# Two tiles for the turned residual, other places for two rounded sums, and filling that is counted from the first head

## The chip, the cores and the metric

The program runs on one core of one Trainium2 chip. The time is device microseconds of one execution, from the first to the last instruction with what lies around them. Before the change three runs gave 1033.18, 1035.9 and 1036.19 us, with a median of 1035.9.

## The reference, cut to what matters

Two layers over 512 tokens of width 1024, in float32: attention, an MLP, a recurrent block, an MLP, and a last norm. Every part is a residual branch behind an RMS norm.

```python
def sq_relu_mlp(h, w1, w2):
    z = jax.nn.relu(jnp.einsum('bsd,df->bsf', h, w1))
    return jnp.einsum('bsf,fd->bsd', z * z, w2)

for layer in range(DEPTH):
    hn = rmsnorm(h, norm_mix[layer])
    mix = chunked_band_attention(hn, ...) if layer % 2 == 0 else rglru_block(hn, ...)
    h = h + mix
    h = h + sq_relu_mlp(rmsnorm(h, norm_mlp[layer]), mlp_w1[layer], mlp_w2[layer])
return rmsnorm(h, norm_final)
```

With 512 tokens in chunks of 64 and eight chunks to the left, attention's band is the whole past: 16 heads of width 64, a bias per head by clipped distance, a softmax, and the output projection. The MLP goes up to 4096 and back.

## The kernel before

**Products in three parts.** Each float32 operand is split into a rounded high part (float32r) and what is left, and each product is made of three matmuls (`mm3`, lines 288 to 290). ScalarE casts the high part (for weights line 179, tiles wh), VectorE subtracts it for the low part (line 184, tiles wl). Weights come by DMA through a few raw tiles and a ring of five split tiles.

**Attention (lines 364 to 640).** The residual lies transposed: eight tiles of 128 features by 512 tokens. A loop runs over the heads: `score` (the two matmul lines 483 and 484, bias, maximum, exponent, scaling), one head later `turn` (ten transposes on TensorE, line 514), and another head later `weigh` (lines 529 and 530). Scores, transposes and the first two value tiles take turns in four PSUM banks with the tag "at". Between these three stands other matmul work: a queue of value, query and key projections and of the output projection, cut into steps of three matmuls. `fill(n)` adds n to a credit that may carry over at most 3, and takes steps from the queue while the credit is above 0; each step costs 2. `need` takes steps without regard to the credit where a head cannot do without a projection. Before the loop, 17 steps are taken directly. A key projection ends with `k_out`, which splits the key and copies it to the other 64 partitions by DMA on SP (lines 401 and 402).

**The MLP (`mlp`, line 681).** It uses products of 2 x 2 blocks with fewer multiplications, in Winograd's manner: sums of blocks of the weights (made on VectorE, or by accumulating DMAs that GpSimd issues) against sums of blocks of the input. At the start, `first` does four plain up tiles (`up`, j = 0 to 3), 24 matmuls of 512 columns each. Beside them:

- after the first tile, `turn` transposes the residual in 32 x 32 blocks on VectorE (line 744, 16 instructions) into the tile `turned`, and 32 DMAs (line 751, 16 on SP, 16 on GpSimd's queue) write it to `res`, where tokens lie on partitions;
- after the second, ScalarE scales the residual in its place by the norm's gain (line 697);
- after the third, `right` makes four sums of blocks of it (lines 701 to 705);
- after the fourth, `right_split` rounds them into rH (line 714, ScalarE) and rL (line 715, VectorE).

Then `group` runs seven products of 24 matmuls of 256 columns: the first on the plain operand (hnH, hnL), the second, third, fifth and seventh on the sums rH and rL. Between the first and the third stands a copy from PSUM to PSUM on ScalarE (line 850).

**Places.** The tile rH holds all four rounded sums, 16 KB in each partition, and has the tag "rH" that `turned` has: both take turns in one place, so the first cast into rH has to wait until all 32 DMAs have read `turned`. The low parts of sums 2 and 4 lie in the place of the residual's lower half, which sums 1 and 3 are read from. The two halves of a "22" block of the down weights have 8 KB under the tag "b22" and are loaded in `load_down`.

**Order.** A scheduler places the instructions on the engines by its own estimate of times, within what data and places allow; each engine and each DMA queue then works strictly in that order.

Of the kernel before, what the change touches and what calls it, by code (L numbers as in the profile page):

```python
# [10 lines left out]
F32 = mybir.dt.float32  # L11
F32R = mybir.dt.float32r
# [3 lines left out]
P = 128  # L16
T = 512
D = 1024
KT = D // P
NH = 16  # L20
HD = 64
U = 256
EPS = 1e-6
NEG = -1e30

FILL = 7.6

WARM = 10

# [6 lines left out]
def f(ap):  # L36
    return ap.bitcast(F32)
# [3 lines left out]
def trunk(ctx: ExitStack, tc: tile.TileContext, xT, cols, gfin, win, wqkv, wo, rwin, rga, rgx, rwo, w1, w2, out):  # L41
# [70 lines left out]
    def load_down(key, name):  # L112
        if key not in down:
            return
        both = state["raw"].tile([P, 2, 1024], F32, name=f"b{name}_{key[0]}{key[1]}", tag=f"b{name}")
        for h in range(2):
            raws[name, h] = both[:, h]
            nc.sync.dma_start(two(raws[name, h]), rows(down[key][name][h * U : (h + 1) * U]))
# [19 lines left out]
    def fetch():  # L138
        i = state["next"]
        state["next"] += 1  # L140
        kind, nk, key = plan[i]
        H = wsp.tile([P, 1024], F32R, name=f"wh{i}", tag="wh")
        L = wsp.tile([P, 1024], F32R, name=f"wl{i}", tag="wl")
# [34 lines left out]
        if i:  # L178
            high = S.copy(H[:, :n], raw[:, :n])  # L179
            if kind in ("us1", "us3", "t1", "t4") or kind in ("t2", "t3") and key[1] == 3:  # L180
                tc.keep_in_program_order(high)
        else:
            start_.append(V.tensor_copy(H[:, :n], raw[:, :n]))
        low = V.tensor_sub(L[:, :n], raw[:, :n], f(H[:, :n]))  # L184
        if not i:
# [24 lines left out]
        elif kind == "t4" and half:  # L210
            first_sum(following)
            load_down(following, "22")
            load_down(following, "21")
        state["ready"].append((nk, H[:, :n].rearrange("p (k c) -> p k c", k=nk), L[:, :n].rearrange("p (k c) -> p k c", k=nk)))

# [150 lines left out]
    with ExitStack() as actx:  # L366
# [6 lines left out]
        def bias_of(g):  # L373
            b = ab.tile([P, 4, T], F32, name=f"bias{g}", tag="bias")
            nc.sync.dma_start(b[:, :, 2 * P :], win[4 * g : 4 * g + 4].rearrange("h p j -> p h j"))
            for h in range(4):
                G.tensor_copy(b[:, h, 0 : 2 * P], b[:, h, 2 * P : 2 * P + 1].to_broadcast([P, 2 * P]))
            G.memset(b[0:HD, :, T - HD :], NEG)
            biases[g] = b
# [12 lines left out]
        def k_out(p, acc):  # L392
            tmp = a2.tile([P, T], F32, name=f"tk{p}", tag="tmp")
            V.tensor_mul(tmp, acc, r0)
            for hh in range(2):
                own, oth = HALF[hh], HALF[1 - hh]
                kh = ab.tile([P, T], F32R, name=f"kh{p}{hh}", tag=f"kh{hh}", bufs=2)
                kl = ab.tile([P, T], F32R, name=f"kl{p}{hh}", tag=f"kl{hh}", bufs=2)
                S.copy(kh[own], tmp[own])
                V.tensor_sub(kl[own], tmp[own], f(kh[own]))  # L400
                nc.sync.dma_start(f(kh[oth]), f(kh[own]))
                nc.sync.dma_start(f(kl[oth]), f(kl[own]))
                kk[2 * p + hh] = (kh, kl)
# [69 lines left out]
        def score(h):  # L473
            kh, kl = kk[h]
            s0, s1, s2 = atp(f"s0{h}"), atp(f"s1{h}"), atp(f"s2{h}")
            sc = [s0[:, 0:P], s0[:, P : 3 * P], s1[:, : 3 * P], s2]
            pt = a2.tile([P, 10 * P], F32, name=f"p{h}", tag="p")
            mx = a2.tile([P, 4], F32, name=f"mx{h}", tag="mx")
            sm = a2.tile([P, 4], F32, name=f"sm{h}", tag="sm")
            b = biases[h // 4]  # L480
            for t in range(4):
                n = (t + 1) * P
                PE.matmul(sc[t], q[h][:, t * P : n], kl[:, :n], start=True, stop=False)
                PE.matmul(sc[t], q[h][:, t * P : n], kh[:, :n], start=False, stop=True)
            for t in range(4):
                n = (t + 1) * P
                V.tensor_tensor_reduce(
                    out=pt[:, seg[t] : seg[t] + n], in0=sc[t], in1=b[:, h % 4, T - n :],
                    scale=1.0, scalar=-3.0e38, op0=ALU.add, op1=ALU.max, accum_out=mx[:, t : t + 1],
                )  # L490
            V.tensor_scalar(mx, mx, -1.0, None, ALU.mult)
            for t in range(4):
                n = (t + 1) * P
                S.activation(
                    pt[:, seg[t] : seg[t] + n], pt[:, seg[t] : seg[t] + n], AF.Exp,
                    bias=mx[:, t : t + 1], accum_out=sm[:, t : t + 1],
                )
            V.reciprocal(sm, sm)
            for t in range(4):
                n = (t + 1) * P  # L500
                V.tensor_scalar(pt[:, seg[t] : seg[t] + n], pt[:, seg[t] : seg[t] + n], sm[:, t : t + 1], None, ALU.mult)
            pts[h] = pt
# [90 lines left out]
        credit = [0]  # L593

        def step():
            try:
                credit[0] -= next(queue[0][1])
            except StopIteration:
                queue.pop(0)
# [6 lines left out]
        def need(name):  # L606
            while any(name == item[0] for item in queue):
                step()
# [3 lines left out]
        q_out(1, accs[1])  # L612
        for _ in range(KT):
            step()
        for i in range(NH + 2):
            if i < NH:
                if i % 4 == 0 and i > 0:
                    bias_of(i // 4)
                if i >= 4:
                    need(f"k{i // 2}")  # L620
                score(i)
                if i == 0:
                    k_out(1, accs[3])
                at["s"] = i
            fill(FILL)
            if 0 <= i - 1 < NH:
                turn(i - 1)
            fill(FILL)
            if 0 <= i - 2 < NH:
                if i == 15:  # L630
                    need("woA")
                need(f"v{(i - 2) // 8}")
                weigh(i - 2)
                if i == 9:
                    residual("h")
                    for k in range(KT):
                        nc.sync.dma_start(hT[k], xT[k * P : (k + 1) * P, :])
                at["w"] = i - 2
            fill(FILL)
        need("woB")  # L640
# [40 lines left out]
    def mlp(ly, norm):  # L681
        with ExitStack() as mctx:
            sr, zp, dp = (mctx.enter_context(tc.tile_pool(name=f"{n}{ly}", bufs=1)) for n in ("sr", "z", "d"))
# [2 lines left out]
            xs = [(hnH[k], hnL[k]) for k in range(KT)]  # L686
            res = dp.tile([P, 4, 2, T], F32, name=f"d{ly}", tag="d")
            dt = {(t, c): res[:, t, c] for t in range(4) for c in range(2)}
            turned = zp.tile([P, 2, 2, 4, KT, 32], F32, name=f"turned{ly}", tag="rH")
            rights = []  # L690
            rL13 = zp.tile([P, 2, 4, U], F32R, name=f"rL13{ly}", tag="rL")
            low_, high = hB[0], hB[1]
            rF = {1: low_[:, :, LO], 3: low_[:, :, HI], 4: high[:, :, LO], 2: high[:, :, HI]}
            rL = {1: rL13[:, 0], 3: rL13[:, 1]}
# [10 lines left out]
                    V.scalar_tensor_tensor(rF[n], rF[1 if n == 2 else 2], -1.0, rF[n], ALU.mult, ALU.subtract)  # L705

            def right_split(n):
                if n == 1:
                    rights.append(zp.tile([P, 4, 4, U], F32R, name=f"rH{ly}", tag="rH"))
                if n == 2:  # L710
                    rL24 = per.tile([P, 2, 4, U], F32R, name=f"rL24{ly}", tag="hx0")
                    rL.update({2: rL24[:, 0], 4: rL24[:, 1]})
                H = rights[0][:, n - 1]
                S.copy(H, rF[n])  # L714
                V.tensor_sub(rL[n], rF[n], f(H))  # L715

            def operand(n):
                if n[0] == "r":
                    H, L = rights[0][:, int(n[1]) - 1], rL[int(n[1])]
                    return [(H[:, k], L[:, k]) for k in range(4)]  # L720
                ks, c = (range(4) if n[0] == "1" else range(4, KT)), (LO if n[1] == "1" else HI)
                return [(hnH[k][:, c], hnL[k][:, c]) for k in ks]
# [15 lines left out]


            def turn():  # L740
                blocks = [turned[:, h] for h in range(2)]
                for k in range(KT):
                    for h in range(2):
                        V.transpose(
                            blocks[h].rearrange("p t j k a -> p (t j) k a")[:, :, k],
                            hT[k][:, h * U : (h + 1) * U].rearrange("p (n b) -> p n b", b=32),
                        )
                for h in range(2):
                    for i in range(4):
                        for j in range(4):  # L750
                            (G if j % 2 else nc.sync).dma_start(
                                res[32 * j : 32 * j + 32, 2 * h : 2 * h + 2, i // 2, (i % 2) * U : (i % 2 + 1) * U],
                                blocks[h][32 * i : 32 * i + 32, :, j].rearrange("p t k a -> p t (k a)"),
                            )
# [327 lines left out]
    def open_x(u):  # L1082
        WH, WL = want(1)
        for i in range(2):
            xbs.append(mmp(f"xb{2 * u + i}"))
            project(xbs[-1:], PAIR[i : i + 1], WH, WL, [(hnH[k], hnL[k]) for k in range(4, KT)], last=False)
            yield

    mlp(0, nm1)


    nm2 = Norm("nm2", C_MLP1, late=True)
    with ExitStack() as rctx:
# [142 lines left out]
        for u in range(2, 4):  # L1236
            WH, WL = want(2)
            for i in range(2):
                m = 2 * u + i
                project([accs[m]], PAIR[i : i + 1], WH, WL, [gd[k] for k in range(KT)])  # L1240
                ro_out(m)

    mlp(1, nm2)


# [39 lines left out]
```

## Time and profile before

| | |
|---|---|
| profiled execution | 1035.93 us, its span 1034.2 us |
| granted TensorE clock | 0.999 |
| PE (matmuls) busy | 1021.6 us, 99% |
| VectorE busy | 866.8 us, 84% |
| ScalarE busy | 665.7 us, 64% |
| GpSimd busy | 99.4 us, 10% |
| attention's head loop | about 40 to 229 us of the span |
| first MLP, recurrent block, second MLP | from about 244, 555 and 709 us |

PE is TensorE's matmuls, PEld its weight loads, DVE VectorE, ACT ScalarE, POOL GpSimd, SPq the DMA queue of SyncE. A row of a timeline gives the start, the duration, the engine, the line, the operation, the tile written and the tiles read, and in brackets how long the engine stood idle before it and what ended that. Shown durations of matmuls overlap. Tile names stand without their numbers: `m` is a bank of `group`, `s` one of scores, `x` in line 514 one of transposes, `v` of values.

### The profile page before, as it was taken

How to read it: one execution, taken by the hardware profiler on the slowest of the kernel's cores; microseconds unless marked ns; L12 is line 12 of the kernel's file. 1: busy time of each engine (PE TensorE's matmuls, PEld its weight loads, DVE VectorE, ACT ScalarE, POOL GpSimd, SP SyncE). 2: the span in 40 equal slices, each digit the busy share in tenths (PEclk: the TensorE clock that was granted, in tenths of full speed). 3: DMA queues.
4: the chain of work that ended last, by engine and by line, in shares of the span. 5: the costliest groups of instructions: out<-in, count | busy, mean ns of one | idle time of the engine just before them, and what ended most of it. 6: DMA issues, size and time to landing. Idle time of an engine off the chain costs nothing.

```text
span 1034.2 us, 15261 instructions
## 1 busy us (share of the span) xinstructions
PE 1021.6 (99%) x5762; PEld 892.5 (86%) x5762; DVE 866.8 (84%) x1222; ACT 665.7 (64%) x1020; POOL 99.4 (10%) x128
## 2 busy tenths in 40 slices
PE   9999999999999999999999999999999999999997
PEld 7888888888999999999988788888899999999986
DVE  7998778869789898698688989977789698698687
ACT  7676556646787566567567686645786567567565
POOL 1000000003101111111020000012101111111020
PEclk9999999999999999999999999999999999999999
DMA  8444344249648738828773412196648838828572
GB/s 269 120 124 140 84 153 121 74 121 247 173 79 232 208 56 216 218 51 214 205 143 102 123 62 82 43 281 167 159 90 225 217 57 211 223 49 212 142 166 84
DMA packets 125482, 153.62 MB, mean 149 GB/s; under 512 B 6497, under 2 KB 94561, under 8 KB 125409
## 3 DMA queue, kind: packets, MB, share of 16 engines
q1 hardware_dynamic: 102752, 114.18, 35.2%
q0 software_dynamic: 22080, 37.76, 21.1%
q8 instruction: 45, 0.74, 0.3%
q10 hardware_dynamic: 576, 0.72, 0.2%
q14 instruction: 29, 0.23, 0.1%
HBM read 123.27 MB, written 2.10 MB: 121 GB/s over the span
## 4 chain that ended last, share of the span: by engine, by line
PE 82%; DVE 7%; DMA 5%; ACT 2%; SPq 2%; issue 1%; DVEq 0%; ACTq 0%
PE m L289 9%; PE m L288 9%; PE m L290 9%; PE x L288 6%; PE x L289 6%; PE x L290 6%; PE y L288 4%; PE y L289 4%; PE y L290 4%; DVE wl L184 2%; PE x L514 1%; PE v L288 1%; DMA wr<-in_w 1%; PE v L290 1%; PE yb L290 1%; PE v L289 1%
## 5 line engine op out<-in xcount | busy, mean ns | idle before, releaser
L184 DVE TENSOR_TENSOR wl<-b,wh 128x1024 fp32r<-128x1024 f32 x112 | 135.6, 1221 | 31.4 <-ACT wh L179 31.2
L179 ACT CAST wh<-b 128x1024 fp32r<-128x1024 f32 x112 | 116.7, 1051 | 57.7 <-PE x L290 18.8
L289 PE MATMUL m<-rL,wh 128*128 128x256 f32 x448 | 126.2, 282 | 0.9 <-DVE rL L715 0.9
L288 PE MATMUL m<-rH,wh 128*128 128x256 f32 x448 | 126.1, 281 | 1.0 <-ACT rH L714 0.6
L290 PE MATMUL m<-rH,wl 128*128 128x256 f32 x448 | 125.9, 281 | 0.0
L179 ACT CAST wh<-wr 128x1024 fp32r<-128x1024 f32 (+1 forms) x65 | 66.7, 1029 | 47.9 <-PE wo L289 11.8
L290 PE MATMUL m<-hnH,wl 128*128 128x256 f32 x336 | 95.0, 283 | 0.0
L289 PE MATMUL m<-hnL,wh 128*128 128x256 f32 x336 | 95.0, 283 | 0.0
L288 PE MATMUL m<-hnH,wh 128*128 128x256 f32 x336 | 94.9, 282 | 0.0
L184 DVE TENSOR_TENSOR wl<-wr,wh 128x1024 fp32r<-128x1024 f32 (+1 forms) x66 | 78.2, 1188 | 12.3 <-ACT wh L179 11.9
L289 PEld LDWEIGHTS m<-rL,wh 128*128 128x128 f32 x448 | 84.9, 190 | 2.8 <-DVE rL L715 1.5
L288 PEld LDWEIGHTS m<-rH,wh 128*128 128x128 f32 x448 | 84.8, 189 | 2.6 <-ACT m L850 0.8
L290 PEld LDWEIGHTS m<-rH,wl 128*128 128x128 f32 x448 | 84.9, 189 | 0.0
L179 ACT CAST wh<-u 128x1024 fp32r<-128x1024 f32 x56 | 58.0, 1050 | 25.3 <-PE x L290 16.9
L184 DVE TENSOR_TENSOR wl<-u,wh 128x1024 fp32r<-128x1024 f32 x56 | 67.6, 1219 | 2.3 <-ACT wh L179 2.3
L289 PEld LDWEIGHTS m<-hnL,wh 128*128 128x128 f32 x336 | 64.2, 191 | 0.8
L288 PEld LDWEIGHTS m<-hnH,wh 128*128 128x128 f32 x336 | 64.2, 191 | 0.8
L290 PEld LDWEIGHTS m<-hnH,wl 128*128 128x128 f32 x336 | 64.3, 191 | 0.0
L288 PE MATMUL x<-wh,h 128*128 128x512 f32 (+1 forms) x132 | 50.9, 386 | 0.6 <-DVE d L1059 0.6
L290 PE MATMUL x<-wh,l 128*128 128x512 f32 (+1 forms) x132 | 50.9, 385 | 0.0
L289 PE MATMUL x<-wl,h 128*128 128x512 f32 (+1 forms) x132 | 50.7, 384 | 0.0
L288 PE MATMUL y<-wh,hs 128*128 128x512 f32 x128 | 50.2, 392 | 0.0
(384 smaller groups left out, 2892.6 us busy)
## 6 DMA issues: line engine op xcount, KB each, us to landing
b<-in_w SPq DMA_DIRECT2D x68, 512.0 KB, 6.1
b<-b POOLq DMA_DIRECT2D x36, 512.0 KB, 7.0
kept<-in_w SPq DMA_DIRECT2D x28, 512.0 KB, 3.8
u<-in_w SPq DMA_DIRECT2D x28, 512.0 KB, 5.8
wr<-in_wqkv SPq DMA_DIRECT2D x20, 512.0 KB, 4.2
wr<-in_rwin SPq DMA_DIRECT2D x16, 512.0 KB, 3.6
kept<-in_w POOLq DMA_DIRECT2D x14, 512.0 KB, 8.1
u<-in_w POOLq DMA_DIRECT2D x14, 512.0 KB, 7.4
```

The costliest lines, as they stand in the source:

```text
L179: high = S.copy(H[:, :n], raw[:, :n])
L184: low = V.tensor_sub(L[:, :n], raw[:, :n], f(H[:, :n]))
L288: PE.matmul(acc, WH, XH, start=start, stop=False, skip_group_check=more)
L289: PE.matmul(acc, WH, XL, start=False, stop=False, skip_group_check=more)
L290: PE.matmul(acc, WL, XH, start=False, stop=stop, skip_group_check=more)
L514: PE.transpose(b[:, c : c + P], pt[:, seg[t] + kt * P : seg[t] + (kt + 1) * P], ident)
```

## The change

Three things are edited.

1. `credit[0] = 0` stands ahead of the head loop, so the 17 steps taken before it no longer count against the fills, and FILL is 7.4 instead of 7.6.
2. The turned residual has two tiles, one for each half of the tokens. That of the first half (`turned…0`) has the tag "b22", in the place of the down weights' 22 block; that of the second half (`turned…1`) has the tag "rH24". The DMAs of the second half are written first.
3. The rounded sums have two tiles: sums 1 and 3 lie alone ("rH13"), sums 2 and 4 under the tag "rH24", in turn with the second half's turned tile.

```diff
-FILL = 7.6
+FILL = 7.4
...
         for _ in range(KT):
             step()
+        credit[0] = 0
         for i in range(NH + 2):
...
-            turned = zp.tile([P, 2, 2, 4, KT, 32], F32, name=f"turned{ly}", tag="rH")
-            rights = []
+            late = [zp.tile([P, 2, 4, KT, 32], F32, name=f"turned{ly}1", tag="rH24")]
+            rH13 = zp.tile([P, 2, 4, U], F32R, name=f"rH13{ly}", tag="rH13")
+            rH = {1: rH13[:, 0], 3: rH13[:, 1]}
...
             def right_split(n):
-                if n == 1:
-                    rights.append(zp.tile([P, 4, 4, U], F32R, name=f"rH{ly}", tag="rH"))
                 if n == 2:
+                    rH24 = zp.tile([P, 2, 4, U], F32R, name=f"rH24{ly}", tag="rH24")
+                    rH.update({2: rH24[:, 0], 4: rH24[:, 1]})
                     rL24 = per.tile([P, 2, 4, U], F32R, name=f"rL24{ly}", tag="hx0")
                     rL.update({2: rL24[:, 0], 4: rL24[:, 1]})
-                H = rights[0][:, n - 1]
+                H = rH[n]
                 S.copy(H, rF[n])
                 V.tensor_sub(rL[n], rF[n], f(H))
...
             def turn():
-                blocks = [turned[:, h] for h in range(2)]
+                blocks = [sr.tile([P, 2, 4, KT, 32], F32, name=f"turned{ly}0", tag="b22"), late.pop()]
...
-                for h in range(2):
+                for h in (1, 0):
                     for i in range(4):
                         for j in range(4):
                             (G if j % 2 else nc.sync).dma_start(
```

How instructions move is seen on three engines. From line 615 on, the new kernel's line numbers are one or two higher. First TensorE at head 0's last scores (s20) in attention; v02 and v03 are value tiles, s01 to s21 the banks of head 1's scores. Before:

```order
L484 MATMUL s20_487<-kh00_377,q00_369 128x512
L288 MATMUL v02_481<-wh6_249,hnH1_77 128x512
L483 MATMUL s01_527<-kl01_384,q01_372 128x128
L484 MATMUL s01_527<-kh01_383,q01_372 128x128
L483 MATMUL s01_527<-kl01_384,q01_372 128x256
L484 MATMUL s01_527<-kh01_383,q01_372 128x256
```

And now, where head 1's scores begin:

```order
L288 MATMUL v03_552<-wh8_285,hnH4_80 128x512
L289 MATMUL v03_552<-wl8_286,hnH4_80 128x512
L290 MATMUL v03_552<-wh8_285,hnL4_88 128x512
L483 MATMUL s01_568<-kl01_384,q01_372 128x128
L484 MATMUL s01_568<-kh01_383,q01_372 128x128
```

One matmul stood between the two heads' scores, now 36 do: the 21 that are left of v02 and 15 of v03. Further on, 19 projection matmuls stood between the end of the second pair's key projection (qk2k) and head 4's scores, which need that key; now there are 39.

Second, ScalarE in the second MLP, from the cast of the third weight tile of `group` (us2) to the copy of line 850; u102 and u103 are the third and fourth up tile, a000 and a001 their results. Before:

```order
L179 CAST wh174_7095<-u12_10_6801 128x1024
L771 ACTIVATE a000_1_6909<-u102_7008 128x256
L771 ACTIVATE a001_1_6912<-u102_7008 128x256
L772 ACTIVATE a000_1_6909<-a000_1_6909 128x256
L772 ACTIVATE a001_1_6912<-a001_1_6912 128x256
L714 CAST rH1_7077<-t0_5520 128x1024
L771 ACTIVATE a000_1_6909<-u103_7048 128x256
L771 ACTIVATE a001_1_6912<-u103_7048 128x256
L772 ACTIVATE a000_1_6909<-a000_1_6909 128x256
L772 ACTIVATE a001_1_6912<-a001_1_6912 128x256
L714 CAST rH1_7077<-t0_5520 128x1024
L714 CAST rH1_7077<-t1_5521 128x1024 x2
```

Behind these stands the copy of line 850. Now the casts stand around the second up tile u101, followed by weights and the later up tiles:

```order
L179 CAST wh172_7008<-kept01_6875 128x1024
L716 CAST rH131_6873<-t0_5522 128x1024 x2
L773 ACTIVATE a000_1_6912<-u101_6971 128x256
L773 ACTIVATE a001_1_6915<-u101_6971 128x256
L774 ACTIVATE a000_1_6912<-a000_1_6912 128x256
L774 ACTIVATE a001_1_6915<-a001_1_6915 128x256
L716 CAST rH241_7085<-t1_5523 128x1024 x2
L179 CAST wh173_7045<-us2_10_7047 128x1024
L179 CAST wh174_7099<-u12_10_6803 128x1024
```

All four casts of sums stand some ten instructions earlier, those of sums 2 and 4 ahead of two weight casts and of the activations of u102 and u103. Behind these follow the cast of the first down operand (h1110), that of the next weights (wh175) and the copy, now line 852. In the first MLP the two casts of sums 2 and 4 stand on either side of the cast of us2, ahead of the third up tile. On VectorE in the second MLP, seven of the 16 transposes now stand ahead of the last residual tile's sum; before, all 16 stood behind it, and that sum behind a weight split.

Third, SP's queue at the same place. b22 is the 22 block, wr170 the fourth up tile's weights, d1 the tile that the turned residual goes to. Before:

```order
L154 DMA wr169_6789<-in_w1 128x8x128
L118 DMA b22_10_7130<-in_w2 128x2x512 x2
L154 DMA wr170_6795<-in_w1 128x8x128
L134 DMA u11_10_6799<-in_w1 128x4x256
L134 DMA u12_10_6801<-in_w1 128x4x256
L751 DMA d1_6869<-turned1_6870 32x2x256 x16
L134 DMA kept1_7087<-in_w1 128x4x256 x2
```

And now:

```order
L154 DMA wr169_6791<-in_w1 128x8x128
L154 DMA wr170_6797<-in_w1 128x8x128
L134 DMA u11_10_6801<-in_w1 128x4x256
L134 DMA u12_10_6803<-in_w1 128x4x256
L753 DMA d1_6871<-turned10_6918 32x2x256
L753 DMA d1_6871<-turned11_6872 32x2x256 x8
L753 DMA d1_6871<-turned10_6918 32x2x256 x7
L118 DMA b22_10_7134<-in_w2 128x2x512
L134 DMA kept1_7091<-in_w1 128x4x256
```

The two loads of the 22 block move from ahead of wr170 to behind the turned residual's DMAs, and of these one of the first half, then eight of the second half, then the other seven are issued. GpSimd's queue has its 16 in the same order.

More of the change, by code (lines that the diff above doesn't have):

```diff
@@ L718, in operand @@
                 if n[0] == "r":
-                    H, L = rights[0][:, int(n[1]) - 1], rL[int(n[1])]
+                    H, L = rH[int(n[1])], rL[int(n[1])]
                     return [(H[:, k], L[:, k]) for k in range(4)]
```

## The prediction

> **What bounds the kernel now.** I read the page's busy line first, then the table by stretches, then TensorE's own timeline wherever that table leaves it less than full.
>
> ```profile
> span 1034.2 us, 15261 instructions
> PE 1021.6 (99%) x5762; PEld 892.5 (86%) x5762; DVE 866.8 (84%) x1222; ACT 665.7 (64%) x1020; POOL 99.4 (10%) x128
> ...
> 40.00:60.00 20.00, 19.04 (x103) 16.05 (x102) 16.92 (x51) 15.06 (x39) 0.00 (x0) 1.00 0.30 80
> 300.00:320.00 20.00, 20.00 (x130) 18.28 (x129) 19.97 (x21) 13.64 (x18) 3.18 (x4) 1.00 0.83 196
> 720.00:740.00 20.00, 18.34 (x104) 15.67 (x103) 14.45 (x13) 11.19 (x21) 7.42 (x13) 1.00 0.54 118
> ```
>
> In the stretches the columns are length, PE, PEld, DVE, ACT, POOL busy, clock, DMA share, GB/s. TensorE is busy all the time, at full clock, and the number of its matmuls does not change. So the only thing this change can win or lose is the time in which TensorE stands still. Vector at 19.97 of 20 costs nothing in 300 to 320, since PE shows 20.00 beside it. In 40 to 60 and in 720 to 740 PE falls short.
>
> A matmul's shown duration overlaps the next one's, so lost time is read from starts: start to start minus the usual step. Attention first:
>
> ```profile
> 41.03 0.39 PE L484 MATMUL s<-kh,q 128*128 128x512 f32 x1
> 41.26 0.40 PE L288 MATMUL v<-wh,hnH 128*128 128x512 f32 x1
> 42.61 0.30 PE L483 MATMUL s<-kl,q 128*128 128x128 f32 x1 [0.96 <-issue]
> ...
> 78.74 0.45 PE L288 MATMUL qk3q_out<-hnH,wh 128*128 128x512 f32 x1
> 79.94 0.30 PE L483 MATMUL s<-kl,q 128*128 128x128 f32 x1 [0.76 <-DMA kl<-kl]
> ...
> 159.75 0.28 PE L484 MATMUL s<-kh,q 128*128 128x256 f32 x1
> ```
>
> The step of a 512-column matmul is 41.26 - 41.03 = 0.23 us. Head 1's scores start 42.61 - 41.26 - 0.23 = 1.12 us late, head 4's 79.94 - 78.74 - 0.23 = 0.97 us late. The second is named: head 4's key, copied to the other half of the partitions, has not landed. The first is not; the row that ends beside it is this one:
>
> ```profile
> 42.02 0.48 DVE L432 SCALAR_TENSOR_TENSOR v<-v,rt,v 128x256 fp32r<-128x256 f32 x1 [0.34 <-ACT v L431]
> ```
>
> Four PSUM banks are shared by the first two value tiles, scores and transposes. Head 0 takes three, and head 1's first bank is the one that this last reading of the second value tile gives back at 42.5. I take that as the cause. Then the two MLP entries:
>
> ```profile
> 272.35 0.28 PE L290 MATMUL m<-rH,wl 128*128 128x256 f32 x1
> 272.84 0.38 PE L288 MATMUL m<-rH,wh 128*128 128x256 f32 x1 [0.21 <-ACT m L850]
> 273.26 0.38 PE L289 MATMUL m<-rL,wh 128*128 128x256 f32 x1
> ...
> 733.39 0.28 PE L289 MATMUL m<-hnL,wh 128*128 128x256 f32 x1
> 733.51 0.28 PE L290 MATMUL m<-hnH,wl 128*128 128x256 f32 x1
> 734.35 0.38 PE L288 MATMUL m<-rH,wh 128*128 128x256 f32 x1 [0.56 <-ACT rH L714]
> 735.61 0.39 PE L289 MATMUL m<-rL,wh 128*128 128x256 f32 x1 [0.88 <-DVE rL L715]
> ...
> 738.35 0.28 PE L290 MATMUL m<-rH,wl 128*128 128x256 f32 x1
> 738.83 0.38 PE L288 MATMUL m<-rH,wh 128*128 128x256 f32 x1 [0.20 <-ACT m L850]
> 739.24 0.38 PE L289 MATMUL m<-rL,wh 128*128 128x256 f32 x1
> ```
>
> The step of a 256-column matmul is 733.51 - 733.39 = 0.12 us. First MLP: 0.37 + 0.30 = 0.67 us lost. Second: 0.72 + 1.14 + 0.36 + 0.29 = 2.51 us. What ACT does there:
>
> ```profile
> 267.26 1.05 ACT L714 CAST rH<-h 128x1024 fp32r<-128x1024 f32 x1 [3.88 <-DMA u<-in_w]
> 268.21 0.65 ACT L771 ACTIVATE a<-u 128x256 f32<-128x256 f32 x2
> ...
> 269.37 2.94 ACT L714 CAST rH<-h 128x1024 fp32r<-128x1024 f32 x3
> 272.20 0.59 ACT L850 COPY m<-m 128x512 f32<-128x512 f32 x1
> ...
> 733.25 1.05 ACT L714 CAST rH<-t 128x1024 fp32r<-128x1024 f32 x1 [4.72 <-DMA d<-turned]
> ```
>
> In the second MLP the first rounded sum rH waits 4.72 us for the turned residual's DMAs, because rH is written over the tile that they read. In the first MLP the profile names another DMA, but the program lets this cast wait only for the same reading. PE then waits for rH, for rL behind it, and for the copy L850, which stands behind all four casts on ACT.
>
> **The change part by part.** *The credit.* The 17 steps taken before the head loop leave a debt of 34, so the first four fills of 7.6 do nothing: head 1's scores stand one matmul behind head 0's. With the debt cleared 36 matmuls lie between, 36 x 0.23 = 8.3 us, against the 1.35 us (42.61 - 41.26) after which the bank was free. That takes away the 1.12 us. The 17 steps come earlier everywhere after: between the end of the second pair's key projection and head 4's scores stood 19 projection matmuls (4.4 us), now 39 (9.0 us), with the work of a head in both. The copied key was 0.97 us late; it gets 4.6 us more. That takes away 0.97. Together 2.09 us.
>
> *7.4 instead of 7.6* takes 54 x 0.2 / 2 = 5 steps out of the loop's fills; they are forced later or run after it, so no matmul goes away. What it costs is bounded by a place that is packed tightly now: head 11's scores right behind other transposes. Its rows are the 159.75 above and
>
> ```profile
> 160.08 0.44 PE L483 MATMUL s<-kl,q 128*128 128x384 f32 x1
> ```
>
> where a step of 0.12 took 0.33, so 0.2 us is lost at one such wait. After the change head 5's scores come only one weighing behind head 3's transposes, head 15's no longer come tightly. Ends: one tight place fewer (-0.2) to three more waits (+0.6) somewhere in 16 heads; I take +0.6, as the order is new for a whole stage.
>
> *The turned tile.* No transpose, cast or DMA is added; 32 DMAs per MLP are issued as before, but those of the second half of the tokens go ahead, behind one of the first half. Sums 1 and 3 get a place of their own, so their casts need no DMA at all: they move ahead of the second up tile's activations on ACT. Sums 2 and 4 lie over the second half's tile and wait for its 16 DMAs. The tile of the first half lies in the place of the 22 block of the down weights, whose two loads now wait for the other 16.
>
> ```profile
> L751 SPq DMA_DIRECT2D d<-turned x16: 594/602/898, 251.4 to 261.7; - x16
> L751 POOL DMA_DIRECT2D d<-turned x16: 547/566/588, 252.0 to 260.1; - x16
> DMA to landing us min/median/max: 2.1/2.8/5.1
> ...
> L751 SPq DMA_DIRECT2D d<-turned x16: 588/598/2040, 716.8 to 728.2; - x16
> L751 POOL DMA_DIRECT2D d<-turned x16: 539/540/588, 717.5 to 725.5; - x16
> DMA to landing us min/median/max: 2.0/2.9/5.2
> ```
>
> The numbers are ns per issue (min/median/max), then the first and last start. SP is the slower queue. Nine issues have gone at 251.4 + 9 x 0.60 = 256.8, landed at 259.6, by the slowest landing 261.9. Second MLP: 716.8 + 9 x 0.60 = 722.2, landed 725.1, at the slowest 727.4.
>
> Is that early enough? This is the step that could go wrong, since ACT runs in order and the casts of sums 2 and 4 now stand ahead of weight casts, activations and L850. From the first of them to the end of L850 lie two casts of a sum (0.98 each, 2.94 / 3), four casts of 1.05 (three of weights, one of the first down operand), two groups of four activations (269.37 - 268.21 = 1.16 each) and L850's 0.59: 1.96 + 4.2 + 2.32 + 0.59 = 9.1 us. PE needs L850's result at 272.35 + 0.12 = 272.5, and in the second MLP at 733.51 + 25 x 0.12 = 736.5. So the casts may start as late as 263.4 and 727.4. Margins: 3.8 and 2.3 us at the median landing, 1.5 and none at the slowest. In the second MLP there is more, by these rows:
>
> ```profile
> 708.21 1.05 ACT L179 CAST wh<-wr 128x1024 fp32r<-128x1024 f32 x1 [3.01 <-DMA wr<-in_w]
> 709.29 1.23 DVE L184 TENSOR_TENSOR wl<-wr,wh 128x1024 fp32r<-128x1024 f32 x1 [3.31 <-ACT wh L179]
> ...
> 310.11 1.05 ACT L179 CAST wh<-b 128x1024 fp32r<-128x1024 f32 x1 [0.26 <-ACT wh L179]
> ```
>
> Vector, with the transposes behind it, stood 3.31 us for a weight load that was queued behind the 22 block's 1 MB on SP. That megabyte is now queued after the turned DMAs, and seven transposes move into the gap, so the DMAs start up to 3 us earlier. The 22 block is first cast at 310.11 in the first MLP; loaded after its tile is read (267 plus a load of about 6 us) it is there at 273, 37 us early: cost 0. SP's kept loads stand behind it, but they too waited for the sums' casts before (they were issued at 740 in the second MLP), so nothing new waits. I take the 0.67 and the 2.51 as removed: 3.18 us; ends 0 and 3.18, below that the rival.
>
> There is a rule against this. The Trainium skill (SBUF — State Buffer, "SBUF: two separate sides") says that DMAs issued by GpSimd stall while Vector runs in its two-port mode, because their descriptors cannot be written. By that rule the sum would be rival C's. The trace disagrees: no POOL issue took over 588 ns, with Vector's fp32 work running beside it.
>
> **Sum.** 2.09 + 3.18 - 0.6 = 4.7 us. The profiled execution took 1035.93 us, the median of the runs shown is 1035.9, so nothing has to be converted: 1035.93 - 4.7 = **1031.2 us**.
>
> **Rivals.** *A, attention gives its gain back.* Vector is 16.9 of 20 busy in 40 to 60, and earlier projections ask it for weight splits and keys sooner; if such waits return all 2.09 us besides the 0.6, only 3.18 - 0.6 = 2.6 remains: 1033.3. For it: both attention stalls hung on Vector's lateness. Against: the debt had crowded two heads into one stretch, and filling from the first head spreads Vector's work.
> *B, the MLP entries find another wait,* such as the u block's DMA that the profile names at 267.26: 2.09 - 0.6 = 1.5 us won, 1034.4.
> *C, POOL's half of the DMAs comes late.* If each POOL issue had to wait out a Vector instruction of 1.23 us, nine would end at 263.1 and 728.6, landed 265.9 and 731.5: 2.5 and 4.1 us past the points above, 6.6 lost for 5.27 removed, with the 0.6 1037.9.
> *D, ACT blocks, and it ends slower.* If the second half's DMAs land no earlier than rH could start before (267.26 and 733.25, for instance because the accumulating loads hold them up), L850 ends 9.1 us later, at 276.4 and 742.4: 3.9 and 5.9 us lost. 9.8 + 0.6 - 5.27 = 5.1 us slower, 1041.0. It decides from the point where the two delays beyond 263.4 and 727.4 add up to 4.7. Against it: these DMAs now go first.
> *E, nothing,* if the stalls differ by execution and the profiled one shows them larger than most: 1035.9. One of the three runs took 1033.18, 2.7 less than the others, so some of what I remove may not always be there.
>
> **How the numbers follow.** Chances: forecast 0.63, A 0.13, B 0.07, C 0.04, D 0.07, E 0.06. A measurement of this kernel tells no less than about 0.3% from no change, 3.1 us: below 1032.8 is faster, above 1039.0 slower. The forecast lies 1.6 us inside; I give 0.04 of it to "same" and 0.05 of A to "faster": faster 0.64. Slower is D, with 0.01 of C and 0.02 of E by the scatter of the runs: 0.10. The rest is 0.26. The range: at best the +0.6 does not come, another us of small waits goes, and a comparison falls 1 to 2 us lower as the one run did: 1028; above it takes in A and B and stops at 1035.5, which leaves out C, D and half of E, and a little below.
>
> **What would show it.** Right: head 1's first score starts 0.23 after its predecessor; no wait for "DMA kl<-kl" before head 4; the first matmul on rH in both MLPs 0.12 after the last one on hnH, and the casts of sums 1 and 3 long before 267 and 733, with those of 2 and 4 before 263 and 727. Wrong: ACT's wait for "DMA d<-turned" longer than before, L850 late again, or new gaps before scores or transposes between 50 and 200.

## The result, and the profile after

The changed kernel takes 1032.53 us in the median of 22 runs (1031.87 to 1033.43), the kernel before 1035.12 us in 22 runs beside it (1033.18 to 1038.78). The ratio is 0.9975, with a 95% interval of 0.9969 to 0.9982: 2.6 us less. The interval excludes no change, but the gain stays below the 0.3% that the prediction set as its bound. It is a little over half of the 4.7 us forecast. The scatter fell too, from 5.6 us to 1.6 us.

The profiled execution took 1033.43 us. This is its busy line, and then its table by stretches with the columns named in the prediction:

```profile
span 1031.6 us, 15285 instructions
PE 1020.6 (99%) x5762; PEld 893.8 (87%) x5762; DVE 866.3 (84%) x1222; ACT 666.1 (65%) x1020; POOL 100.3 (10%) x128
```

```profile
40.00:60.00 20.00, 20.00 (x100) 16.92 (x100) 15.99 (x42) 13.99 (x31) 0.00 (x0) 0.95 0.48 132
720.00:740.00 20.00, 20.00 (x126) 18.13 (x125) 16.62 (x15) 12.95 (x23) 5.35 (x8) 0.95 0.86 217
```

TensorE is full in both stretches in which it fell short before. The clock column shows 0.95 in this execution; its steps from matmul to matmul are still 0.12 and 0.23 us, so I read nothing from it.

**The MLP entries** on TensorE's timeline:

```profile
269.83 0.28 PE L290 MATMUL m<-hnH,wl 128*128 128x256 f32 x1
269.95 0.28 PE L288 MATMUL m<-rH,wh 128*128 128x256 f32 x1
...
733.62 0.28 PE L290 MATMUL m<-hnH,wl 128*128 128x256 f32 x1
733.74 0.28 PE L288 MATMUL m<-rH,wh 128*128 128x256 f32 x1
733.86 0.28 PE L289 MATMUL m<-rL,wh 128*128 128x256 f32 x1
```

The first matmul on rH follows the last one on hnH after 0.12 us in both MLPs, and the one on rL follows after 0.12 us: no wait is left. ScalarE shows why:

```profile
253.85 2.00 ACT L716 CAST rH<-h 128x1024 fp32r<-128x1024 f32 x2
260.11 1.05 ACT L716 CAST rH<-h 128x1024 fp32r<-128x1024 f32 x1 [2.44 <-DMA d<-turned]
262.01 1.04 ACT L716 CAST rH<-h 128x1024 fp32r<-128x1024 f32 x1
270.33 0.59 ACT L852 COPY m<-m 128x512 f32<-128x512 f32 x1
...
717.68 2.00 ACT L716 CAST rH<-t 128x1024 fp32r<-128x1024 f32 x2
722.82 2.00 ACT L716 CAST rH<-t 128x1024 fp32r<-128x1024 f32 x2 [1.36 <-DMA d<-turned]
734.11 0.59 ACT L852 COPY m<-m 128x512 f32<-128x512 f32 x1
```

Sums 1 and 3 are cast early. Sums 2 and 4 still wait for the turned residual's DMAs, 2.44 and 1.36 us, but at 260.1 and 722.8, ahead of the latest harmless starts of 263.4 and 727.4. The wait is there, and nothing waits for it.

**Attention** has lost its two named waits and found others. This is the list of what TensorE waited for (total, times, longest), cut to attention:

```profile
PE s L483 <- DVE pL L519: 1.1, 1, 1.1
...
PE s L483 <- DMA kl<-kl: 1.0, 1, 1.0
...
PE x L514 <- DVE mx L487: 0.4, 1, 0.4
```

And the timeline of TensorE at head 1's first score, at head 5's and at head 12's:

```profile
49.49 0.39 PE L290 MATMUL v<-wh,hnL 128*128 128x512 f32 x1
49.72 0.22 PE L483 MATMUL s<-kl,q 128*128 128x128 f32 x1
...
87.48 0.28 PE L484 MATMUL s<-kh,q 128*128 128x256 f32 x1
88.85 0.45 PE L483 MATMUL s<-kl,q 128*128 128x384 f32 x1 [1.09 <-DVE pL L519]
...
177.04 0.39 PE L289 MATMUL qk7k_out<-hnL,wh 128*128 128x512 f32 x1
178.43 0.30 PE L483 MATMUL s<-kl,q 128*128 128x128 f32 x1 [0.99 <-DMA kl<-kl]
```

Head 1 starts 0.23 us after its predecessor, so its 1.12 us are gone, and so are head 4's 0.97 us. But head 5's third bank comes 88.85 - 87.48 - 0.12 = 1.25 us late, head 12's key 178.43 - 177.04 - 0.23 = 1.16 us late, and head 13's transposes lose 0.58 us near 198. VectorE and SP ahead of the two larger waits:

```profile
86.98 1.22 DVE L184 TENSOR_TENSOR wl<-wr,wh 128x1024 fp32r<-128x1024 f32 x1
88.11 1.28 DVE L519 TENSOR_TENSOR pL<-x,pH 128x512 fp32r<-128x512 f32 x2
...
171.47 1.22 DVE L184 TENSOR_TENSOR wl<-wr,wh 128x1024 fp32r<-128x1024 f32 x1
172.60 0.68 DVE L541 TENSOR_TENSOR oL<-o,oH 128x512 fp32r<-128x512 f32 x1
173.21 1.40 DVE L400 TENSOR_TENSOR kl<-tk,kh 64x512 fp32r<-64x512 f32 x2
174.07 1.16 SPq L402 DMA_DIRECT2D kl<-kl  x2
```

The bank is released by a subtraction (L519) that stands behind a weight split of 1.22 us; the key by a subtraction (L400) behind a weight split and another subtraction, and its copy lands 4 us later. VectorE goes from one to the next without a pause: it is late.

For the comparisons below I add up, over each stage, start to start minus a fixed usual step (0.2265, 0.1755, 0.119 and 0.100 us for 512, 384, 256 and 128 columns); a shorter step counts against the sum. Attention runs from the first score to the first up tile of the MLP, an MLP entry is the 45 us from its first up tile. The table gives the us lost by TensorE, from one profiled execution of each kernel; the last two kernels come with the experiments:

| kernel | attention | first entry | second entry |
|---|---|---|---|
| before | 8.45 | 1.06 | 2.81 |
| changed | 8.64 | 0.13 | 0.15 |
| MLP's edits alone | 8.28 | 0.16 | 0.14 |
| attention's edit alone | 8.65 | 0.16 | 1.58 |

Attention holds 5 to 5.6 us of losses below 0.15 us each in all four. Kernels with the same order of attention on TensorE agree within 0.2 us. Before and after differ by 0.2 us in attention and by 3.6 us in the entries. To the start of the last matmul the profiles differ by only 1027.7 - 1025.2 = 2.5 us, because the profile after happens to lose 0.28 us more before attention and 0.47 us more in the recurrent stage (3.28 us, against 2.75 to 2.83 in the other profiles), which the change doesn't touch.

### The profile page after: what moved, and what is told of

Its sections match the earlier page's. It is cut to its first block, busy times and chain, and to the rows that moved or that the text cites. A ratio compares the mean times of both kernels' runs of the same rounds, so it can differ in the third digit from the quotient of the medians.

```text
span 1031.6 us, 15285 instructions
## 1 busy us (share of the span) xinstructions
PE 1020.6 (99%) x5762; PEld 893.8 (87%) x5762; DVE 866.3 (84%) x1222; ACT 666.1 (65%) x1020; POOL 100.3 (10%) x128
## 3 DMA queue, kind: packets, MB, share of 16 engines
q0 software_dynamic: 22080, 37.76, 21.2%
## 4 chain that ended last, share of the span: by engine, by line
PE 91%; DVE 6%; ACT 2%; issue 1%; DMA 0%; DVEq 0%; POOL 0%; SPq 0%; ACTq 0%; POOLq 0%
PE m L290 9%; PE m L289 9%; PE m L288 9%; PE x L288 6%; PE x L289 6%; PE x L290 6%; PE y L288 4%; PE y L289 4%; PE y L290 4%; PE ro L290 1%; PE ro L289 1%; PE ro L288 1%; PE v L288 1%; PE yb L288 1%; PE v L290 1%; PE v L289 1%
## 5 line engine op out<-in xcount | busy, mean ns | idle before, releaser
L288 PEld LDWEIGHTS m<-rH,wh 128*128 128x128 f32 x448 | 84.8, 189 | 1.0
```

Source lines behind the costliest of these rows:

```text
L288: PE.matmul(acc, WH, XH, start=start, stop=False, skip_group_check=more)
```

## The experiments

Two theories were to be told apart after the result. Theory 1: VectorE, in order and 165 of the 200 us from 40 to 240 busy, is late in attention, so whatever order the heads have, the waits move and the sum stays. The rival: the order itself makes the waits, so a better count of filling steps takes them away. Each kernel was timed beside the kernel before on the same chip; "lost" is the sum above. The stretch from 40 to 240 in the kernel before, and in the changed one (VectorE is the third busy time):

```profile
40.00:240.00 200.00, 198.03 (x1018) 166.89 (x1017) 164.81 (x392) 122.51 (x271) 7.20 (x16) 1.00 0.42 119
40.00:240.00 200.00, 197.48 (x1017) 167.52 (x1017) 164.86 (x394) 123.33 (x271) 8.04 (x16) 0.95 0.41 118
```

### Each part alone

The MLP's edits alone: the changed kernel with attention as before.

```diff
-FILL = 7.4
+FILL = 7.6
-        credit[0] = 0
```

> The MLP edits alone (two turned tiles, other places for the sums); the credit and 7.6 as before. Theory 1 (the whole gain is TensorE's standing still at the two MLP entries, and the attention edit only moved its waits to other heads): about 1035.1 - 3.2 = 1031.9 us, thus no slower than the full change; TensorE full in the first 30 us of both MLPs, and attention's two waits of 1.1 and 1.0 us still there. Theory 2 (each edit gave about half of the 2.6 us): 1033.8 us. If the scatter of the kernel before (1033.2 to 1038.8) came from the turned tile's DMAs, this one's runs lie within 1.5 us of each other.

Measured: 1032.37 us against 1034.81, ratio 0.9975 (0.9965 to 0.9985). The second part alone is the kernel before with the reverse of that diff:

> The attention edit alone (credit set to 0, 7.4 instead of 7.6), the MLPs as before. Theory 1: 1035.1 us, between 1034.5 and 1036; the waits of heads 1 and 4 gone, waits of about 1.2 us each at heads 5 and 12 in their place; MLP entries lose 0.7 and 2.5 us as before. Theory 2: 1033.8 us. Scatter as wide as before if it came from the turned tile's DMAs, narrow if it came from attention's waits.

Measured: 1034.53 us against 1034.81, ratio 1.000 (0.9991 to 1.0009). Lost in attention: 8.65 us, with the same waits at the same places as in the changed kernel (1.60 us at 87.2, 1.27 at 177.0, 0.60 at 197.5; here and below a wait's place is the start of the matmul ahead of it). So the MLP's edits alone give the whole gain, 2.4 us, and attention's edit is worth nothing that can be measured: its interval reaches 0.9 us to either side. The narrower scatter comes with the MLP's edits too: their nine runs lie within 1.2 us, those of attention's edit alone within 2.3 and those of the kernel before within 2.8.

In this second kernel the old MLP lost only 1.74 us in its entries, against 3.87 us in before's profile. The order of instructions on ScalarE, VectorE and SP is the same at both entries of these two kernels, so what the old place of rH costs differs from execution to execution. These are the first casts of a sum in this second kernel:

```profile
266.34 1.05 ACT L715 CAST rH<-h 128x1024 fp32r<-128x1024 f32 x1 [2.67 <-DMA d<-turned]
731.38 1.05 ACT L715 CAST rH<-t 128x1024 fp32r<-128x1024 f32 x1 [3.20 <-DMA u<-in_w]
```

They start 21.2 and 23.0 us after the first up tile (at 245.1 and 708.4), and 22.4 and 24.3 us after it in before's profile (267.26 and 733.25, with up tiles from 244.8 and 709.0). The DMAs that let them start came 1.2 us earlier; why is not shown.

### The order of the two halves' DMAs

The change also issues the second half's DMAs first. Here the first half goes first, with all else as changed.

```diff
-                for h in (1, 0):
+                for h in (0, 1):
```

> The full change, but the DMAs of the first half of the tokens are written first again, so the second half's tile, under sums 2 and 4, is read last. The casts of sums 2 and 4 can then start only at about 264.5 and 727 (16 issues of 0.6 us and 2.8 us to land) instead of 260.1 and 722.8. Theory 1 (margins of 3 us and more were to spare, and the scheduler puts these casts later on ScalarE): within 0.5 us of the full change, no wait at the MLP entries over 0.3 us. Rival (the order of the halves is what makes the two places work): 1.5 to 3 us slower than the full change, with ScalarE waiting for the turned tile's DMAs and the copy of line 852 late.

Measured: 1032.05 us, ratio 0.9977 (0.9966 to 0.9987); lost in the entries 0.16 and 0.14 us. The casts of sums 2 and 4 start at 263.2 and 726.9 there, three and four us later than in the changed kernel, and the scheduler put them behind the third up tile's activations; the copy of line 852 still starts at 270.6 and 733.8. The order of the halves is worth nothing that can be measured; the two places are enough.

### Other counts of filling steps

The full change with 7.6 and with 8.0 instead of 7.4 (FILL alone).

> The full change with 7.6 kept: only the credit is reset. Theory 1 (any change of the filling deals the heads' places anew, and each order has its own few waits of 0.5 to 1.3 us): 1031.5 to 1033.5 us, with waits at heads other than 5 and 12 or of other sizes. Rival (the new waits come from the smaller fills, 7.4): they vanish, 1030.5 us.

> The full change with fills of 8.0, four whole steps each time: the filling is the same at every head, and no forced steps crowd heads 10 to 13 together. Theory 1 (any order has its few waits, because VectorE is late at some place in any of them): 1031.5 to 1033 us, the stage still loses 8 us and more. Rival (the crowding of heads after forced steps is the cause): heads 11 and 12 wait no longer, 1.2 us less than the full change, though more filling in the loop leaves less for the last heads.

Measured: 1032.18 us, ratio 0.9974 (0.9964 to 0.9984), with 8.90 us lost in attention; and 1032.19 us, ratio 0.9975 (0.9966 to 0.9985), with 8.77 us. With 7.6 the waits above 0.3 us stand at 60.0, 87.6, 177.3 and 226.6; with 8.0 at 84.8, 87.5, 156.2, 174.4 and 225.8. The sum hardly changes, 8.3 to 8.9 us for four different orders. The places change less than theory 1 has it: with the credit reset, heads 5 and 12 keep large waits with every count (1.25 and 1.16 us with 7.4, 1.51 and 1.29 with 7.6, 1.01 and 0.74 with 8.0), and the other waits move. This speaks against the rival, as far as the counts tried go; these three orders are much alike, and no quite different one was tried.

### What held head 1

The prediction took the second value tile's bank as the cause of head 1's wait. Here, in the kernel before, that tile takes a bank of another tag, so that it no longer shares the scores' four.

```diff
-                acc = (atp if g == 0 and t < 2 else mmp)(f"v{g}{t}")
+                acc = (atp if g == 0 and t < 1 else mmp)(f"v{g}{t}")
```

> The kernel before, with one edit: the second value tile takes its PSUM bank from the other group of four (tag mm), so that head 1's scores have a free bank at once. If the prediction's cause for head 1's wait was right (the bank that the last reading of that value tile gives back), the 1.13 us at 41 us is gone or moves to the next use of these banks. If the wait was something else, it stays. Time, theory 1 (a wait removed in attention comes back at another place): 1034.0 to 1035.5 us, the stage's lost time still 8 to 9 us; rival (waits add up singly): 1.1 us faster than before. The MLP entries are those of the kernel before, and show how much they lose in one more execution: 3.9 us in the first profile, 1.7 us in that of the attention edit alone.

Measured: 1035.67 us against 1034.87, ratio 1.0007 (0.9997 to 1.0017), 0.2 us above the range that theory 1 gave. TensorE and VectorE at head 1:

```profile
40.45 0.39 PE L484 MATMUL s<-kh,q 128*128 128x512 f32 x1
40.68 0.22 PE L483 MATMUL s<-kl,q 128*128 128x128 f32 x1
...
41.03 0.28 PE L484 MATMUL s<-kh,q 128*128 128x256 f32 x1
42.66 0.45 PE L483 MATMUL s<-kl,q 128*128 128x384 f32 x1 [1.35 <-DVE mx L487]
```

The first score now starts at once, 0.23 us after its predecessor: the cause was named rightly. But two matmul pairs later TensorE waits 42.66 - 41.03 - 0.12 = 1.51 us, for VectorE's reading of head 0's scores (L487). The bank was only the first thing in a row that VectorE had not finished; lost in attention 8.64 us.

### VectorE's work up and down

Three kernels take work from VectorE: the softmax division of the two longer row blocks of each head goes to ScalarE, in the changed kernel, in the one with 8.0, and in the one with the MLP's edits alone. A fourth gives VectorE an unused copy of 128x512 for each head.

```diff
-                V.tensor_scalar(pt[...], pt[...], sm[:, t : t + 1], None, ALU.mult)
+                if t < 2:
+                    V.tensor_scalar(pt[...], pt[...], sm[:, t : t + 1], None, ALU.mult)
+                else:
+                    S.activation(pt[...], pt[...], AF.Copy, scale=sm[:, t : t + 1])
```

```diff
             pts[h] = pt
+            V.tensor_copy(wk.tile([P, T], F32, name=f"idle{h}", tag="nsq", bufs=2), hnH[0].bitcast(F32))
```

> The changed kernel, with the softmax division of the two longer row blocks (128x384 and 128x512) of each head moved from VectorE to ScalarE. In the changed kernel's profile these are 32 of the 64 multiplications of line 501, which last 279 to 622 ns; about 1.1 us a head, 17 us in all, leave VectorE, which is busy 164.9 of the 200 us from 40 to 240; ScalarE, busy 123.3 of them, takes on about 18 to 20. Theory 1 (attention's stalls on TensorE are VectorE running late, so any order of the heads moves them and none removes them): attention loses at least 1.5 us less, 1031.0 us or below. Rival (the order of the work on TensorE makes them, or the score banks are too few): attention loses what it lost, 1032.1 to 1032.9. A second rival: ScalarE becomes the late one, since the division stands behind its exponentials and its casts; then a new wait for it, and the time is 1033 or above.

> The same move on the kernel that counts 8.0 filling steps for a head (1032.19). Theory 1: again 1.5 us or more faster, 1030.7 or below, near the run with 7.4, since with VectorE early the count of steps matters little. Rival of the order: 1031.8 to 1032.6.

> The changed kernel with one more VectorE copy of 128x512 in each of the 16 heads, its result unused: about 0.4 to 0.7 us each, some 6 to 11 us of VectorE in all, and nothing moved on TensorE. Theory 1: the waits of the heads that were late grow by about the copy or more, since the lateness adds up over the in-order queue: 1 us or more slower, 1033.5 us or above. Rival of the order: VectorE has 35 of 200 us free, the copies fall into them, 1032.1 to 1032.9.

> The kernel with the MLP's edits alone (heads counted as before, 1032.37), and the same move of the division to ScalarE. Theory 1: the old waits of heads 1 and 4 shrink or go with VectorE's relief, 1.5 us or more faster, 1030.9 or below: then the order of the heads is not needed for it. Rival of the order: head 1's wait, which hangs on VectorE's reading of two value tiles at the stage's start and not on the division, stays at about 1.1 us and head 4's too, 1032.0 to 1032.7.

| kernel | us | ratio to before | lost in attention, its base |
|---|---|---|---|
| changed, division on ScalarE | 1031.45 | 0.9966 (0.9953 to 0.9978) | 7.10, 8.64 |
| 8.0, division on ScalarE | 1033.33 | 0.9984 (0.9975 to 0.9993) | 9.54, 8.77 |
| MLP's edits, division on ScalarE | 1032.95 | 0.9980 (0.9971 to 0.9989) | 9.57, 8.28 |
| changed, copies on VectorE | 1034.20 | 0.9993 (0.9984 to 1.0002) | 10.46, 8.64 |

**More work for VectorE** is the clean test: the sequence of TensorE's instructions is that of the changed kernel, row for row. It came out as theory 1 said, and its interval does not touch the changed kernel's (0.9969 to 0.9982). The copies didn't fall one to a head, though. They depend on nothing that a head makes, and the scheduler put all 16 at the start. VectorE and TensorE:

```profile
36.79 0.42 DVE L503 COPY idle<-hnH 128x512 f32<-128x512 f32 x1
39.24 1.09 DVE L503 COPY idle<-hnH 128x512 f32<-128x512 f32 x3
44.27 4.11 DVE L503 COPY idle<-hnH 128x512 f32<-128x512 f32 x12
...
88.41 0.28 PE L484 MATMUL s<-kh,q 128*128 128x256 f32 x1
90.14 0.44 PE L483 MATMUL s<-kl,q 128*128 128x384 f32 x1 [1.46 <-DVE pL L520]
```

By 48.4 they have taken 5.6 us of VectorE's time. Forty us later head 5's wait is 90.14 - 88.41 - 0.12 = 1.61 us instead of 1.25, and new ones of about 0.5 us stand near 52, 69 and 85. From 160 on the waits are those of the changed kernel. VectorE carries a lateness along for about 40 us, and TensorE pays 1.8 us for these 5.6.

**Less work for VectorE** did not do what theory 1 said. The same relief, from 165 to 167 busy us of the 200 to 154 to 156, won 1.5 us of attention once and lost 0.8 and 1.3 us twice. Only with 7.4 does it look like a gain, and there too head 5 still waits 0.80 us and head 12 1.15. The table by stretches of that kernel:

```profile
40.00:240.00 200.00, 198.31 (x1024) 168.26 (x1023) 155.68 (x364) 141.21 (x304) 6.55 (x16) 1.00 0.42 122
```

ScalarE has gone from 123.3 to 141.2 us. The kernel with 8.0 shows a place where that decides. TensorE's order is unchanged up to here; ScalarE, VectorE and TensorE with the division on ScalarE:

```profile
67.68 1.23 ACT L504 ACTIVATE p<-p,sm 128x384 f32<-128x384 f32 x2
68.81 0.83 ACT L521 CAST pH<-x 128x512 fp32r<-128x512 f32 x2
...
69.41 1.02 DVE L522 TENSOR_TENSOR pL<-x,pH 128x512 fp32r<-128x512 f32 x2
...
69.04 0.34 PE L484 MATMUL s<-kh,q 128*128 128x384 f32 x1
70.25 0.47 PE L483 MATMUL s<-kl,q 128*128 128x512 f32 x1 [0.87 <-DVE pL L522]
```

And with 8.0 and the division on VectorE:

```profile
67.38 0.83 ACT L518 CAST pH<-x 128x512 fp32r<-128x512 f32 x2
...
67.97 0.69 DVE L519 TENSOR_TENSOR pL<-x,pH 128x512 fp32r<-128x512 f32 x1 [0.29 <-ACT pH L518]
```

The two divisions stand ahead of the casts of the transposes. The casts start 68.81 - 67.38 = 1.43 us later (0.4 of it lies ahead of attention, whose first score starts at 39.7 instead of 39.3), the subtraction behind them 1.44, and TensorE waits 0.87 us for the bank that this gives back. That is the second rival of the first expectation: ScalarE becomes the late one. In the third kernel head 4's wait is gone, but head 1's stays, 1.46 us at 40.7, as the rival had it: it hangs on VectorE's work before any division. In all three the scheduler also moved work on TensorE at several later places, so how much of their loss is ScalarE and how much the order is not settled.

The first of them has the lowest time of all, and beats both kernels as measured. It is shown faster than the kernel before, by 0.34%; its interval overlaps the changed kernel's, so that it is faster than that one is not shown.

### The keys' low parts on GpSimd

Another relief: the 16 subtractions of L400 (0.69 us each on VectorE) go to GpSimd, in the changed kernel and in the one with 8.0.

```diff
-                V.tensor_sub(kl[own], tmp[own], f(kh[own]))
+                G.tensor_sub(kl[own], tmp[own], f(kh[own]))
```

> The full change, with the low part of each key (16 instructions of 0.7 us, line 400) made by GpSimd in place of VectorE. Theory 1 for why attention gave its gain back: VectorE works in order at 17 to 18 of 20 us there, so that the keys and the low parts of the weights stand behind each other, and the late one is what TensorE waits for. Then taking 11 us of work from it takes the wait of head 12 (1.2 us, key late) and part of that of head 5 (1.25 us): 1 to 2 us faster than the full change, about 1031. Rival (the order of the heads on TensorE alone makes the waits): no faster, as the order of the heads hardly changes. If GpSimd needs more than 2 us for one of them, the keys get later instead and it is slower.

> Fills of 8.0 and the low parts of the keys on GpSimd. If both help by themselves (even filling and a VectorE with less to do), this one is the fastest of all, 1030 us or less; by theory 1 it equals the kernel with GpSimd's keys alone within 0.7 us.

Measured: 1041.02 us against 1034.87, ratio 1.0058 (1.0044 to 1.0072), and 1038.83 us, ratio 1.0039 (1.0027 to 1.0052): slower by 6 and 4 us, with 16.0 and 14.2 us lost in attention. The rows of L400 (minimum, median and longest in ns), and the timeline of GpSimd and VectorE at one of them, in the first of the two:

```profile
L400 POOL TENSOR_TENSOR kl<-tk,kh x16: 1265/1348/2156, 32.4 to 196.8; 64x512 fp32r<-64x512 f32 x16
```

```profile
70.59 3.52 POOL L400 TENSOR_TENSOR kl<-tk,kh 64x512 fp32r<-64x512 f32 x2 [28.03 <-ACT kh L399]
...
71.43 1.55 DVE L184 TENSOR_TENSOR wl<-wr,wh 128x1024 fp32r<-128x1024 f32 x1
72.89 1.25 DVE L491 TENSOR_SCALAR mx<-mx 128x4 f32<-128x4 f32 x1
```

GpSimd takes twice as long, which alone makes the keys late, and VectorE slows beside it: the weight split takes 1.55 us instead of 1.22, and an instruction on four columns, 0.15 to 0.17 us in the changed kernel, takes 1.25 and ends when GpSimd's does (74.1). As a relief of VectorE the test therefore says nothing. It agrees with theory 1 in so far as the largest wait of TensorE in it is again one for VectorE's subtraction:

```profile
PE s L483 <- DVE pL L519: 3.1, 1, 3.1
```

## Why the prediction was right, and where it was wrong

- **The time.** 1032.5 us lies in the range and on the forecast side of before, 1.3 us above the forecast. Part of that closeness is luck: the forecast counts from 1035.93, and the kernel before took 1035.12 in the runs beside the changed one; counted from there it would be 1030.4, 2.1 us below what was measured. The gain is 2.6 us where 4.7 were forecast; "faster by over 0.3%" held most of the chance, and by that bound the result is no difference.
- **The MLP entries, 3.18 us: mechanism right, size perhaps too large.** Casts of sums 1 and 3 early, those of 2 and 4 at 260.1 and 722.8 where 259.6 and 725.1 were worked out, L852 on time, no wait left: each step held. The profiled pair even shows 3.6 us. But the medians give 2.4 us for these edits alone, with an interval of 1.6 to 3.6 us, so 3.18 is not excluded. The term was taken from one execution; the old entries lost 3.87, 1.74 and 3.64 us in three profiles of kernels that had them. Rival E said so for the whole and got a small chance; it may hold for part of this term.
- **The two waits of heads 1 and 4, 2.09 us: removed, as worked out,** and head 1's cause was the bank that was named.
- **"+0.6 for new waits" is the step that failed.** The new waits are 1.25, 1.16 and 0.58 us, 3.0 in all, 0.5 of which stands in place of two small old ones at 177 and 200; with the losses below 0.15 us the term is 2.3. I bounded it by one tightly packed place of 0.2 us and added such places up. The row that bore on it stood in the same part: both old waits hung on VectorE being behind, and moving matmuls does not take work from VectorE.
- **Rival A is what happened,** with its mechanism. Its price was 2.09 + 0.6 = 2.7 us of waits; measured 2.3. Its gain of 2.6 us is the measured one, if not term by term: it had 3.18 from the MLPs less 0.6 in attention, where the parts alone measured 2.4 and 0.3. New gaps before scores between 50 and 200 were also one of the prediction's own signs of being wrong. Against A I had argued that filling from the first head spreads VectorE's work. It does take some from the first stretch (16.92 us busy of 20 from 40 to 60 before, 15.99 after), but none from the stage: VectorE's busy time from 40 to 240 is 164.8 us before and 164.9 us after.
- **B, C and D did not come.** No other wait appeared at the entries. No DMA issue of the turned residual on GpSimd took over 588 ns, so C's price was never due. The prediction said that the trace disagrees with the rule behind C, which the Trainium skill (SBUF — State Buffer, "SBUF: two separate sides") states for VectorE's two-port mode; it doesn't show that. What VectorE ran beside these issues were instructions with two input tensors (TENSOR_TENSOR and SCALAR_TENSOR_TENSOR), and no run here shows the mode of an instruction. ScalarE did wait for the second half's DMAs, 2.44 and 1.36 us, but early enough by 3.3 and 4.6 us.
- **The cause behind A** is shown in one direction: more work on VectorE, with TensorE's sequence held, makes attention lose more. That less work makes it lose less is not shown; it did once and failed twice, since ScalarE became late at one place that I could name and the order moved at others.

## What to carry to other kernels

When a stall on TensorE ends with a late engine that works in order, ask which of that engine's work the change takes away (here none: 2.09 us of waits went and 2.3 came). If none, price the stall as moved, not as removed, and expect it back at the next place where TensorE needs that engine. A wait that hangs on a shared place is different: giving the two users a place each removed it in every profile, and most of the scatter of the runs with it. And a stall read from one execution is one draw: where the runs scatter by more than the gain, look for the same stall in a second profile before its whole size goes into the sum.

## What the hardware showed that I had not expected

GpSimd's subtraction of 64x512 elements takes 1.27 to 2.16 us where VectorE takes 0.69, and VectorE's own instructions are held up beside it, to the point that one of 0.16 us lasts 1.25 and ends together with GpSimd's. The Trainium skill (SBUF — State Buffer, "Who interferes with whom") says that VectorE and GpSimd share one pair of ports and that whichever takes it first keeps it for its whole instruction; the rows above agree. The same page's warning about DMAs issued by GpSimd while VectorE is in its two-port mode (rival C) is neither borne out nor contradicted here: each of the 32 issues in the changed kernel's profile took 539 to 588 ns, and no run shows whether VectorE was in that mode.
